# Where the folded sums of a feed-forward layer's last down run are added: behind the last split pair of the loop, with mixed and plain pairs alternating to the end

## The chip, the cores and the metric

The kernel runs on one core of a Trainium2 chip. Five engines take part, each with its own list of instructions that it works through in order: TensorE (PE; its weight loads are shown apart as PEld), VectorE (DVE), ScalarE (ACT), GpSimd (POOL, which here mainly issues accumulating loads) and SyncE (SP, which issues most loads). Data lies in SBUF; matmuls accumulate in eight PSUM banks of 128 x 512 float32 each. The metric is the device time of one execution in microseconds, lower is better. The kernel before took 1833.16 us, the median of three runs (1832.65 to 1834.87).

## The reference

One layer of an encoder on 256 tokens of width 2048, all in float32: a feed-forward layer, a mixer (a gated recurrence and windowed attention side by side), and a second feed-forward layer. The change lies in the feed-forward layers, which the reference computes twice with different weights:

```python
def rms_norm(x, gain):
    xf = x.astype(jnp.float32)
    y = xf * lax.rsqrt(jnp.mean(xf * xf, axis=-1, keepdims=True) + EPS)
    return (y * gain.astype(jnp.float32)).astype(x.dtype)

def swiglu(x, w_gate_up, w_down):
    gate, up = jnp.split(x @ w_gate_up, 2, axis=-1)
    return (jax.nn.silu(gate) * up) @ w_down
...
    ff = swiglu(rms_norm(x, pre_norm_ffn1[layer]), w_ffn1_gate_up[layer], w_ffn1_down[layer])
    x = x + 0.5 * rms_norm(ff, post_norm_ffn1[layer])
    ...
    ff = swiglu(rms_norm(x, pre_norm_ffn2[layer]), w_ffn2_gate_up[layer], w_ffn2_down[layer])
    x = x + 0.5 * rms_norm(ff, post_norm_ffn2[layer])
```

The inner width is 5632, so the down projection multiplies 256 x 5632 with 5632 x 2048.

## The kernel before

Each float32 operand is held as two parts, h (a rounded copy, made by a cast on ScalarE, line 176) and l (what is left, a subtraction on VectorE, line 177). A product is three matmuls: h with h, h with l, l with h. Making h and l of half a weight tile is called a split here; the split of one half is one cast of 128 x 1024 and one subtraction of 128 x 1024.

The down projection is done in two runs, one for each half of the 2048 output columns. In a run the four blocks of the result (two halves of the tokens times two halves of 1024 columns) stay in four PSUM banks, c (two named pa, two named pb). The 5632 rows of the weight matrix are taken as 22 pairs of 128 rows, numbered 0 to 21. A plain pair takes 8 products (24 matmuls) and two splits. A mixed pair (the even ones from 0 to 18) is multiplied by a scheme of seven products in place of eight: 21 matmuls, but three splits of 1024, one of 512, sums of weight blocks on VectorE (lines 1262 and 1263) and sums of the left operand (tile sp). Four of its seven products go to four further banks, p, for all mixed pairs of a run together. Behind the last mixed pair of a run the sums of p have to be added to the banks c. This is the fold: one copy on ScalarE (line 528) and eight additions on VectorE (lines 529, 522, 523 and 526 make the sums; 535, 539, 543 and 545 add them to the four banks). A later matmul into a bank has to wait for that bank's addition.

Most of the feed-forward layer stands inside a manual schedule: the instructions of each engine keep the order of the source. A table of pair numbers for each run (line 1199) gives the order of the pairs. In a step of the loop (lines 1321 to 1340) the next pair's splits stand ahead of this pair's products on ScalarE and VectorE (`splits`, line 1240); accumulating loads for a mixed pair are issued by POOL four steps ahead (`prepare`, line 1230); a raw weight tile is loaded again by SP as soon as its last split is done (`load_down`, line 1213). Splits write into a ring of five buffers for h and five for l, which come free when TensorE has used them.

The last two pairs of the second run, 20 and 21, are held: `finish` (line 707) loads and splits them into buffers of their own (the pool `post`), and then takes their products bank by bank, so that the norm of the first bank's results can start while the others are computed. This part up to the products is outside the manual schedule; there a scheduler places the instructions. In the first feed-forward layer `finish` also loads and splits the first two weight tiles of the next stage (`lead`, w_mix_in).

In the kernel before, the second run ends with the pairs 16, 1, 18, 17, 19 and then 20, 21. The last mixed pair is 18. The pair behind it, 17, is taken bank by bank, and the fold stands behind 17 and ahead of 19 (`play`, below). `Pairs` also serves the mixer's output projection, with other tables; there nothing changes.

Of the kernel before, what the change touches and what calls it, by code (L numbers as in the profile page):

```python
# [37 lines left out]
def hymba_layer_kernel(  # L38
# [37 lines left out]
    def nm(s):  # L76
        uid[0] += 1
        return f"{s}_{uid[0]}"
# [62 lines left out]
    def load(src, between=None, pool=rawp, **kw):  # L141
        raw = pool.tile([P, 2048], F32, tag="raw", name=nm("raw"), **kw)
        if len(src.shape) == 4:

            dst = raw.rearrange("p (a n b) -> p a n b", a=src.shape[1], n=src.shape[2])
            parts = [(dst[:, a], src[:, a]) for a in range(src.shape[1])]
        else:
            parts = [(raw.rearrange("p (a b) -> p a b", a=src.shape[1]), src)]
        for i, (to, of) in enumerate(parts):
            if i and between:  # L150
                between()
            nc.sync.dma_start(to, of)
        return raw

    def split_load(src, hp=hip, lp=lop, between=None, middle=None):
        return split(load(src, between), hp, lp, middle)

    def split(raw, hp=hip, lp=lop, middle=None):
        hs, ls = [], []
        for i in range(2):  # L160
            if i and middle:
                middle()
            h, l = split_half(raw, i, hp, lp)
            hs.append(h)
            ls.append(l)
        return hs, ls
# [31 lines left out]
    def close_far():  # L198
        far["cm"].__exit__(None, None, None)
# [132 lines left out]
    class LeadN:  # L332


        def __init__(self, w, c0, slot):
            self.w, self.c0, self.slot = w, c0, slot
# [259 lines left out]
    class Pairs(Blocks):  # L596
# [3 lines left out]

        HELD = 2
        firsts = 2

        def __init__(self, w, orders, tiles, sums, room, gain_src, keep=(), near=()):

# [94 lines left out]
        def second_run(self):  # L700
# [3 lines left out]
                    self.gains(m, n)  # L704
            self.run(1)

        def finish(self, mul, post, new_x=None, gain=None, lead=None):


            order = self.orders[1]  # L710
            n_order = len(order)
            self.post = post
            self.work(n_order - self.HELD)
            held = []
            for u in order[n_order - self.HELD :]:
                held.append((u, *split_load(self.source(u), hp=post, lp=post)))
            close_far()
            self.half_gain(post)
            if new_x:
# [4 lines left out]
            r = [None, None]  # L724
# [142 lines left out]
    NU = DFF // 256  # L867
# [139 lines left out]
    def ffn(gated, w_dn, post_gain, again, gain=None, lead=None, aside=None):  # L1007

        with ExitStack() as st:
# [108 lines left out]
            def some(steps, n):  # L1118
                for _ in range(n):
                    next(steps)  # L1120
# [61 lines left out]
            def pair_ahead(g, u):  # L1182
# [16 lines left out]
            orders = [  # L1199
                [9, 11, 8, 13, 10, 15, 12, 1, 0, 3, 14, 5, 16, 17, 2, 7, 4, 19, 6, 18, 20, 21],  # L1200

                [2, 7, 4, 9, 6, 11, 8, 13, 10, 12, 15, 0, 5, 14, 3, 16, 1, 18, 17, 19, 20, 21],
            ]
            added = {0: (12, 0, 14, 16, 2, 4, 6, 18), 1: (2, 4, 6, 10, 12, 0, 14, 16, 18)}
            steps = [(r, u) for r in range(2) for u in orders[r]][: 2 * NU - Pairs.HELD]
            in_order = sorted(
                (i - 3.5 if u in added[r] else i, i) for i, (r, u) in enumerate(steps)
            )
# [1 line left out]
            raws, firsts, got = {}, {}, {}  # L1210
            rows = None
# [26 lines left out]
                    )  # L1238

            def splits(i):  # L1240
                if i >= len(steps):
                    return
                r, u = steps[i]
                raw = raws[i]
                parts = got[i] = []
                b11, b12, b21, b22 = blocks(raw)
                if u not in MIXED:
                    parts.append(split_half(raw, 0))
                    yield
                    parts.append(split_half(raw, 1))  # L1250
                    load_down(raw)
                    yield
                    return
                four = raw.rearrange("p (i c) -> p i c", i=4)
                if i not in firsts:
                    first_block(i)
                    nc.vector.tensor_tensor(
                        four[:, 0:2], four[:, 0::3], four[:, 1:2].to_broadcast([P, 2, 512]), ALU.add
                    )
                parts.append(split_half(raw, 1))  # L1260
                rows.left_sums_ahead(u)
                nc.vector.tensor_tensor(b22, b11, b22, ALU.add)
                nc.vector.tensor_tensor(b21, b22, b21, ALU.add)
                yield
                parts.append(split_half(raw, 0))
                yield
                parts.append(split_half(raw, 1))
                load_down(raw)
                yield

            def products(i, among=None):
                r, u = steps[i]
                rows.pos = i - r * NU
                del raws[i]
                if u in MIXED:
                    rows.products(u, firsts.pop(i), *got.pop(i))
                else:
                    rows.play(u, *zip(*got.pop(i)), among)
                rows.pos += 1
# [3 lines left out]
            with tc.manual_schedule():  # L1283
                gated.prepare(1, MIXED_IN[0])
                some(gated.splits(1, 0), 2)
                for g in range(1, NG):
                    first_pairs(g, waiting)
                    for u in range(2, last - 1):
                        pair_ahead(g, u)
                    some(gated.splits(g, last), 2)  # L1290
                    if g < NG - 1:
                        gated.prepare(g + 1, MIXED_IN[0])
                    for one in gated.take(g, last - 1):
                        one()
                    boundary(g, gated.splits(g + 1, 0) if g < NG - 1 else splits(0))
                    waiting = units(gated.c, rest)
                    some(waiting, 2)
                room_cm.__exit__(None, None, None)
                close_far()
                back_cm = tc.tile_pool(name=nm("hb"), bufs=AWAY // 2, reuse_waits="tile")  # L1300
                back = back_cm.__enter__()
                fetch_at = {2: (1,), 3: (0,), 5: (3,), 6: (5,), 9: (2,), 10: (7,), 11: (4,), 13: (6,)}
                fetch_at.update({25: (0,), 26: (5,), 28: (3,), 29: (1,)})
                again_at = {8: 16, 14: 18}
                for u in MIXED[8:]:
                    sums[u] = None
                rows = Pairs(w_dn, orders, hts, sums, work, post_gain, near=MIXED[:2])
                rows.firsts = 3
                some(waiting, 2)
                ahead = splits(1)  # L1310
                some(ahead, 2)
                products(0)
                for _ in range(2):
                    load_down(back.tile([P, 2048], F32, tag="raw", name=nm("raw"), bufs=2))
                some(waiting, 1)
                ahead = splits(2)
                some(ahead, 2)
                some(waiting, 1)
                some(ahead, 1)
                products(1)  # L1320
                for i in range(2, len(steps)):
                    if i == NU + 18:
                        back_cm.__exit__(None, None, None)
                        early_cm.__exit__(None, None, None)
                        post = rows.post = st.enter_context(post_pool())
                    ahead = splits(i + 1)
                    next(ahead, None)
                    prepare(i + 4)
                    for u in fetch_at.get(i, ()):
                        fetch(u)  # L1330
                    next(ahead, None)
                    products(i)
                    for _ in ahead:
                        pass
                    if i in again_at:
                        sums[again_at[i]] = sums_again(again_at[i])
                    if i == 8:
                        rows.half_gain(far["pool"])
                    if i == NU - 1:
                        rows.second_run()  # L1340
            return rows.finish(
                mul=0.5, post=post, new_x=again, gain=gain and gain(), lead=lead
            )
# [8 lines left out]
    with tc.manual_schedule():  # L1352
# [9 lines left out]
        raw = rawp.tile([P, 2048], F32, tag="raw", name=nm("raw"))  # L1362
# [23 lines left out]
        raws = [load(gated.source(1))]  # L1386
# [97 lines left out]
    with ExitStack() as s2:  # L1484
# [398 lines left out]
        orders = [[0, 1, 4, 6, 5, 7, 2, 3], [0, 4, 1, 5, 6, 7, 2, 3]]  # L1883
        rows = Pairs(w_mix_out[0], orders, yt, ysums, yroom, post_norm_mix)
        rows.half_gain(far["pool"])
        rows.first_run()
        post = s2.enter_context(post_pool())
# [81 lines left out]
```

## Time and profile before

| | |
|---|---|
| median of three runs | 1833.16 us |
| profiled execution | 1832.72 us |
| its span, first to last instruction | 1830.9 us |
| PE busy | 1812.4 us, 99% of the span |
| PEld busy | 1503.5 us, 82% |
| DVE busy | 1599.2 us, 87% |
| ACT busy | 1130.9 us, 62% |
| POOL busy | 155.5 us, 8% |
| granted TensorE clock, mean | 0.998 |
| DMA | 444.45 MB, mean 243 GB/s |

The profile is that of one execution, whose time is 0.44 us under the median; the 1.8 us between its time and its span lie ahead of the first and behind the last instruction. Busy time of PE is time with a matmul in flight, so 99% tells only that it seldom stood empty. In a row of a timeline the first number is the start in microseconds from the span's start, the second the length; a number in brackets is how long the engine had been idle before, with what ended the wait. Lines are those of the kernel before; behind the change the same statements stand on lines up to 24 higher.

### The profile page before, as it was taken

Reading aid. Unit: us, or ns where it says so; the run is one execution under the profiler, and the core shown is the slowest. Engines: PE = TensorE matmul, PEld = TensorE weight load, DVE = VectorE, ACT = ScalarE, POOL = GpSimd, SP = SyncE. Lnnn points to the kernel's source line nnn. Section 1 sums busy time; section 2 is a strip of 40 time slices with the busy share of each in tenths; the row PEclk is TensorE's granted clock in tenths of the full one; section 3 lists DMA queues with packets and bytes.
Section 4 is the critical chain, followed back from the end, with each engine's and each line's share of the span. In section 5 each row is a group of like instructions: output and inputs, shape, how many; then the busy total and the mean of one; then the engine's idle time right before and its main releaser. Section 6 shows DMA issues by size and latency. Waiting matters only on the chain.

```text
span 1830.9 us, 23436 instructions
## 1 busy us (share of the span) xinstructions
PE 1812.4 (99%) x8438; PEld 1503.5 (82%) x8438; DVE 1599.2 (87%) x2041; ACT 1130.9 (62%) x1496; POOL 155.5 (8%) x149
## 2 busy tenths in 40 slices
PE   9999999999999999999999999999999999999997
PEld 6888888888888887888888888788888888888886
DVE  7999999999989988477687798899999999998986
ACT  6565666665656666476587556556666666566663
POOL 1011111111011100000000000001111111011110
PEclk9999999999999999999999999999999999999999
DMA  8789999998698985555554456789999888699892
GB/s 301 230 231 289 275 280 255 252 262 242 231 341 267 301 263 192 187 191 165 169 166 150 170 210 245 218 244 266 282 273 270 255 245 253 199 345 290 272 328 106
DMA packets 210420, 444.45 MB, mean 243 GB/s; under 512 B 11656, under 2 KB 46560, under 8 KB 209536
## 3 DMA queue, kind: packets, MB, share of 16 engines
q1 hardware_dynamic: 180032, 385.14, 60.2%
q0 software_dynamic: 30272, 57.82, 18.2%
q8 instruction: 66, 1.08, 0.2%
q14 instruction: 50, 0.41, 0.1%
HBM read 430.31 MB, written 12.60 MB: 242 GB/s over the span
## 4 chain that ended last, share of the span: by engine, by line
PE 89%; DVE 4%; ACT 3%; DMA 2%; issue 2%; POOL 0%; SPq 0%; DVEq 0%; ACTq 0%; POOLq 0%
PE pa L441 39%; PE pb L441 33%; PE pa L309 5%; PE pa L314 3%; PE pa L364 2%; PE pa L363 2%; PE pa L362 2%; DVE l L177 2%; DMA raw<-in_w_ffn_gate_up_dram 2%; ACT h L176 1%; PE pa L1100 1%; PE pb L1100 1%; PE pb L1690 0%; PE pb L1664 0%; PE pb L1768 0%
## 5 line engine op out<-in xcount | busy, mean ns | idle before, releaser
L176 ACT CAST h<-raw 128x1024 fp32r<-128x1024 f32 (+1 forms) x861 | 851.0, 1013 | 467.6 <-PE pb L441 154.5
L177 DVE TENSOR_TENSOR l<-raw,h 128x1024 fp32r<-128x1024 f32 (+1 forms) x861 | 983.8, 1173 | 140.2 <-ACT h L176 106.0
L441 PE MATMUL pa<-h,xt 128*128 128x512 f32 x1104 | 387.9, 392 | 0.1
L441 PE MATMUL pb<-h,xt 128*128 128x512 f32 x952 | 340.7, 392 | 0.5 <-DVE pb L1152 0.4
L441 PEld LDWEIGHTS pa<-h,xt 128*128 128x128 f32 x1104 | 207.2, 188 | 44.2 <-DVE xt L232 0.6
L441 PE MATMUL pa<-l,xt 128*128 128x512 f32 x552 | 216.0, 391 | 0.1
L441 PEld LDWEIGHTS pb<-h,xt 128*128 128x128 f32 x952 | 178.7, 188 | 43.6 <-DVE pb L1159 3.9
L441 PE MATMUL pb<-l,xt 128*128 128x512 f32 x476 | 185.6, 390 | 0.0
L441 PE MATMUL pa<-h,ht 128*128 128x512 f32 x464 | 163.1, 390 | 3.8 <-DVE pa L535 3.8
L441 PE MATMUL pb<-h,ht 128*128 128x512 f32 x464 | 163.0, 390 | 0.0
L936 POOL DMA_DIRECT2D raw<-in_w_ffn_gate_up_dram x76 | 92.0, 1211 | 738.5 <-DVE l L177 647.0
L309 PE MATMUL pa<-xt,h 128*128 128x512 f32 x512 | 124.5, 393 | 0.2 <-ACT h L176 0.2
L441 PEld LDWEIGHTS pa<-l,xt 128*128 128x128 f32 x552 | 103.8, 188 | 21.5 <-DVE l L177 1.7
L309 PEld LDWEIGHTS pa<-xt,h 128*128 128x128 f32 x512 | 93.8, 188 | 18.6 <-ACT h L176 0.6
L441 PE MATMUL pa<-h,xs 128*128 128x512 f32 x304 | 108.9, 389 | 0.0
L441 PE MATMUL pb<-h,xs 128*128 128x512 f32 x304 | 106.0, 389 | 0.0
L441 PEld LDWEIGHTS pa<-h,ht 128*128 128x128 f32 x464 | 87.1, 188 | 22.6 <-issue 4.6
L441 PEld LDWEIGHTS pb<-l,xt 128*128 128x128 f32 x476 | 89.5, 188 | 17.0
L441 PEld LDWEIGHTS pb<-h,ht 128*128 128x128 f32 x464 | 87.1, 188 | 18.0
L441 PE MATMUL pa<-l,ht 128*128 128x512 f32 x232 | 90.4, 390 | 0.0
L441 PE MATMUL pb<-l,ht 128*128 128x512 f32 x232 | 90.3, 389 | 0.0
L1234 POOL DMA_DIRECT2D raw<-in_w_ffn_down_dram x34 | 41.2, 1211 | 366.2 <-DVE la L177 345.9
(287 smaller groups left out, 2550.8 us busy)
## 6 DMA issues: line engine op xcount, KB each, us to landing
raw<-in_w_ffn_gate_up_dram SPq DMA_DIRECT2D x350, 512.0 KB, 5.8
raw<-in_w_ffn_down_dram SPq DMA_DIRECT2D x88, 1024.0 KB, 7.9
raw<-in_w_mix_in_dram SPq DMA_DIRECT2D x52, 1024.0 KB, 4.9
raw<-in_w_ffn_gate_up_dram POOLq DMA_DIRECT2D x76, 512.0 KB, 8.4
raw<-in_w_ffn_down_dram POOLq DMA_DIRECT2D x34, 512.0 KB, 10.1
raw<-in_w_mix_out_dram SPq DMA_DIRECT2D x16, 1024.0 KB, 5.0
ht<-away SPq DMA_DIRECT2D x24, 512.0 KB, 10.5
away<-ht SPq DMA_DIRECT2D x16, 512.0 KB, 6.8
```

The lines of the kernel that those rows point to most:

```text
L176: nc.scalar.copy(hi, src)
L177: nc.vector.tensor_tensor(lo, src, hi.bitcast(F32), ALU.subtract)
L309: nc.tensor.matmul(slot[f], weights(hs, kk, f), xcol(xt, k), start=(k == 0), stop=(k == KT - 1))
L314: nc.tensor.matmul(slot[f][:, 0:T], weights(ls, kk, f), xcol(xt, kh * 8 + kk, 0), start=False, stop=False,)
L362: nc.tensor.matmul(dst, xh, h[:, o : o + n], start=(k == 0), stop=False)
L363: nc.tensor.matmul(dst, xh, l[:, o : o + n], start=False, stop=False)
L364: nc.tensor.matmul(dst, xl, h[:, o : o + n], start=False, stop=(k == KT - 1))
L441: nc.tensor.matmul(self.bank(at), lhs, rhs, start=(n == 1), stop=n in (ends, self.of[at]), skip_group_check=n > ends,)
L936: nc.gpsimd.dma_start(raw[:, 0:1024].rearrange("p (k c) -> p k c", k=2), self.source(u, g)[:, :, 1], accum_op=ALU.add,)
L1100: nc.tensor.transpose(bank[:, o : o + P], zs[m][:, k * P : (k + 1) * P], ident)
L1234: nc.gpsimd.dma_start(raws[i][:, 0:1024].rearrange("p (k c) -> p k c", k=2), Pairs.part(w_dn, u, r)[:, :, 512:1024], accum_op=ALU.add,)
```

## The change

Three things are changed, all in the second down run of the feed-forward layers. The table of the second run is rewritten so that mixed and plain pairs alternate to the end (10, 15, 12, 5, 0, 3, 14, 1, 16, 17, 18, 19). With 18 in the place before last of the loop, pair 19 is the one taken bank by bank, and the fold stands behind pair 19, ahead of the held pairs. And the held pairs join the loop's list of loads, and their splits get fixed places inside the manual schedule (`hold`): those of pair 20 ahead of pair 18's products, those of pair 21 inside the fold, behind the addition to the first bank.

```diff
+        def hold(self, n, raw=None):
+
+            self.held = self.held or []
+            order = self.orders[1]
+            for _ in range(n):
+                u = order[len(order) - self.HELD + len(self.held)]
+                raw = raw or load(self.source(u))
+                self.held.append((u, *split(raw, hp=self.post, lp=self.post)))
+                raw = None
+
+        def fold_after(self, pos):
+
+            self.after = pos
+            self.rest = 6 * (len(self.order) - pos - 1)
...
             self.work(n_order - self.HELD)
-            held = []
-            for u in order[n_order - self.HELD :]:
-                held.append((u, *split_load(self.source(u), hp=post, lp=post)))
+            if self.held is None:
+                self.hold(self.HELD)
+            held = self.held
...
-                [2, 7, 4, 9, 6, 11, 8, 13, 10, 12, 15, 0, 5, 14, 3, 16, 1, 18, 17, 19, 20, 21],
+                [2, 7, 4, 9, 6, 11, 8, 13, 10, 15, 12, 5, 0, 3, 14, 1, 16, 17, 18, 19, 20, 21],
...
-            steps = [(r, u) for r in range(2) for u in orders[r]][: 2 * NU - Pairs.HELD]
+            steps = [(r, u) for r in range(2) for u in orders[r]]
...
             def splits(i):
-                if i >= len(steps):
+                if i >= 2 * NU - Pairs.HELD:
                     return
...
-                for i in range(2, len(steps)):
+                for i in range(2, 2 * NU - Pairs.HELD):
...
                     next(ahead, None)
+                    if i == NU + 18:
+                        rows.hold(1, raws[2 * NU - 2])
                     products(i)
...
                     if i == NU - 1:
                         rows.second_run()
+                        rows.fold_after(NU - Pairs.HELD - 1)
+                fold = rows.fold()
+                some(fold, 2)
+                rows.hold(1, raws[2 * NU - 1])
+                for _ in fold:
+                    pass
```

The three places at which this is seen in the built program are given for the first layer; in the second the same rows stand in the same order, without the next stage's loads.

VectorE around the fold, before. The tile raw_4212 holds pair 17, raw_635 pair 19, raw_5873 pair 20 and raw_5883 pair 21; y is the buffer of the sums, pa_5107 and pa_5108 are the first two banks c.

```order
L177 TENSOR_TENSOR l_5777<-raw_4212,h_5776 128x1024
L177 TENSOR_TENSOR l_5807<-raw_635,h_5806 128x1024
L177 TENSOR_TENSOR l_5876<-raw_5873,h_5875 128x1024
L177 TENSOR_TENSOR l_5811<-raw_635,h_5810 128x1024
L529 TENSOR_TENSOR y_5838<-pb_5127,y_5838 128x512
L177 TENSOR_TENSOR l_5880<-raw_5873,h_5879 128x1024
L522 TENSOR_TENSOR y_5838<-pb_5128,y_5838 128x512
L177 TENSOR_TENSOR l_5886<-raw_5883,h_5885 128x1024
L523 TENSOR_TENSOR y_5838<-pa_5126,y_5838 128x512
L526 TENSOR_TENSOR y_5838<-pa_5126,y_5838 128x512
L535 TENSOR_TENSOR pa_5107<-pa_5107,y_5838 128x512
L539 TENSOR_TENSOR pa_5108<-pa_5108,y_5838 128x512
```

VectorE there after the change, from pair 18's last split on; raw_629 holds pair 18 and then pair 21, raw_632 pair 19, raw_635 pair 20.

```order
L177 TENSOR_TENSOR l_5802<-raw_629,h_5801 128x1024
L177 TENSOR_TENSOR l_5812<-raw_632,h_5811 128x1024
L177 TENSOR_TENSOR l_5816<-raw_632,h_5815 128x1024
L177 TENSOR_TENSOR l_5820<-raw_635,h_5819 128x1024
L177 TENSOR_TENSOR l_5824<-raw_635,h_5823 128x1024
L529 TENSOR_TENSOR y_5872<-pb_5127,y_5872 128x512
L522 TENSOR_TENSOR y_5872<-pb_5128,y_5872 128x512
L523 TENSOR_TENSOR y_5872<-pa_5126,y_5872 128x512
L526 TENSOR_TENSOR y_5872<-pa_5126,y_5872 128x512
L535 TENSOR_TENSOR pa_5107<-pa_5107,y_5872 128x512
L177 TENSOR_TENSOR l_5880<-raw_629,h_5879 128x1024
L177 TENSOR_TENSOR l_5884<-raw_629,h_5883 128x1024
```

The five additions up to L535 now stand together, with the splits of 19 and 20 ahead of them and those of 21 behind; L539, L543 and L545 follow these.

TensorE at the bank whose addition is L535, before: the last products of pair 17 (ht_3557), then the first of pair 19 (ht_3902), which wait for L535.

```order
L441 MATMUL pb_5110<-h_5776,ht_3557 128x512
L441 MATMUL pb_5110<-l_5777,ht_3557 128x512
L441 MATMUL pb_5110<-h_5776,ht_3557 128x512
L441 MATMUL pa_5107<-h_5806,ht_3902 128x512
L441 MATMUL pa_5107<-l_5807,ht_3902 128x512
L441 MATMUL pa_5107<-h_5806,ht_3902 128x512
```

And after: the last products of pair 19, then the first of pair 20 (ht_4242), which now wait for L535.

```order
L441 MATMUL pb_5110<-h_5815,ht_3902 128x512
L441 MATMUL pb_5110<-l_5816,ht_3902 128x512
L441 MATMUL pb_5110<-h_5815,ht_3902 128x512
L441 MATMUL pa_5107<-h_5819,ht_4242 128x512
L441 MATMUL pa_5107<-l_5820,ht_4242 128x512
L441 MATMUL pa_5107<-h_5819,ht_4242 128x512
```

The wait moved behind pair 19, that is behind 24 more matmuls than have to come after pair 18.

SP's loads at the end of the run, before (pairs 19, 20, 21, the norm's gain row, then the next stage):

```order
L1218 DMA raw_635<-in_w_ffn_down_dram 128x2x1024
L152 DMA raw_5873<-in_w_ffn_down_dram 128x2x1024
L152 DMA raw_5883<-in_w_ffn_down_dram 128x2x1024
L661 DMA pg_5894<-in_post_norm_ffn_dram 128x1024
L152 DMA raw_5899<-in_w_mix_in_dram 128x4x512
```

And after:

```order
L1234 DMA raw_632<-in_w_ffn_down_dram 128x2x1024
L1490 DMA X_5894<-in_x_dram 128x2048
L1234 DMA raw_635<-in_w_ffn_down_dram 128x2x1024
L662 DMA pg_5892<-in_post_norm_ffn_dram 128x1024
L1234 DMA raw_629<-in_w_ffn_down_dram 128x2x1024
L152 DMA raw_5897<-in_w_mix_in_dram 128x4x512
```

The gain row moved ahead of pair 21's load, and half of the reload of X stands between the loads of 19 and 20. Pair 21 is loaded into the tile of pair 18 in both programs, so its load waits for pair 18's last split; behind pair 18 came two more pairs of the loop before, and comes one now. The next stage's first two loads wait for the last splits of 19 and 20, before for those of 19 and of 20 as well; its third waits for pair 21's.

More of the change, by code (lines that the diff above doesn't have):

```diff
@@ L602, in hymba_layer_kernel @@
         firsts = 2
+        held = None
         def __init__(self, w, orders, tiles, sums, room, gain_src, keep=(), near=()):
```

## The prediction

> **What bounds the kernel now.** I read the page's busy times first, then TensorE's waits, then TensorE's own timeline at the longest of them. Page and waits:
>
> ```profile
> span 1830.9 us, 23436 instructions
> ```
>
> ```profile
> PE pa L441 <- DVE pa L535: 3.8, 2, 1.9
> ```
>
> ```profile
> 594.00:687.00 93.00, 93.00 (x412) 77.06 (x411) 81.84 (x87) 59.91 (x68) 8.48 (x7) 1.00 0.89 284
> ```
>
> The second fence is a stretch of the first feed-forward layer's second down run: length, then busy time (instructions) of PE, PEld, DVE, ACT, POOL, then TensorE's clock, the DMA engines' share and GB/s. TensorE is busy for all 93 us. So the middle of the run offers nothing; only the wait on L535 does, once per feed-forward layer, 1.9 us each. L535 adds the first folded sum to bank (0,0); ahead of it stands pair 17, behind it pair 19. TensorE's rows around it, in both layers:
>
> ```profile
> 687.12 0.39 PE L441 MATMUL pb<-l,ht 128*128 128x512 f32 x1
> 687.35 0.39 PE L441 MATMUL pb<-h,ht 128*128 128x512 f32 x1
> 689.66 0.47 PE L441 MATMUL pa<-h,ht 128*128 128x512 f32 x1 [1.92 <-DVE pa L535]
> ...
> 692.50 0.39 PE L441 MATMUL pb<-h,ht 128*128 128x512 f32 x1
> ...
> 1803.42 0.39 PE L441 MATMUL pb<-h,ht 128*128 128x512 f32 x1
> 1805.73 0.47 PE L441 MATMUL pa<-h,ht 128*128 128x512 f32 x1 [1.92 <-DVE pa L535]
> ...
> 1808.55 0.39 PE L441 MATMUL pb<-h,ht 128*128 128x512 f32 x1
> ```
>
> ```profile
> 667.34 2.72 PE pa L441 x12
> ...
> 672.10 1.36 PE pa L441 x6
> ...
> 677.54 2.05 PE pa L441 x9
> ```
>
> Matmuls start 0.23 us apart (687.12 to 687.35), twelve take 2.72 (chain of waits). From the chain's starts a mixed pair takes 672.10 - 667.34 = 4.76 us and a plain pair 677.54 - 672.10 = 5.44.
>
> Why L535 is late, from VectorE's timeline (pair 18's third split to L535), and the same sums in the first run, where no split stands between them:
>
> ```profile
> 673.63 3.65 DVE L177 TENSOR_TENSOR l<-raw,h 128x1024 fp32r<-128x1024 f32 x3
> 678.72 1.23 DVE L177 TENSOR_TENSOR l<-raw,h 128x1024 fp32r<-128x1024 f32 x1 [1.44 <-ACT h L176]
> 680.75 3.50 DVE L177 TENSOR_TENSOR l<-raw,h 128x1024 fp32r<-128x1024 f32 x3 [0.80 <-ACT h L176]
> 684.16 0.69 DVE L529 TENSOR_TENSOR y<-pb,y 128x512 f32<-128x512 f32 x1
> 684.76 1.22 DVE L177 TENSOR_TENSOR l<-raw,h 128x1024 fp32r<-128x1024 f32 x1
> 685.89 0.69 DVE L522 TENSOR_TENSOR y<-pb,y 128x512 f32<-128x512 f32 x1
> ...
> 687.62 0.69 DVE L523 TENSOR_TENSOR y<-pa,y 128x512 f32<-128x512 f32 x1
> ...
> 688.82 0.69 DVE L535 TENSOR_TENSOR pa<-pa,y 128x512 f32<-128x512 f32 x1
> ```
>
> ```profile
> 581.47 0.68 DVE L529 TENSOR_TENSOR y<-pb,y 128x512 f32<-128x512 f32 x1
> ...
> 584.11 0.69 DVE L535 TENSOR_TENSOR pa<-pa,y 128x512 f32<-128x512 f32 x1
> ```
>
> The end of pair 18 to the end of pair 17 is one plain pair, 5.44 us. In it VectorE ran three splits ahead of the sums and two more between them; L529 to the end of L535 took 5.35 us instead of the first run's 3.33.
>
> **The change, part by part.** It removes and adds no instruction; each engine has as many as before.
>
> *The gap.* Ahead of pair 19 both programs have ten mixed and nine plain pairs, so TensorE reaches it at the same time, 687.35 + 0.23 = 687.58, but now waits there for no sum. Gap removed: 689.66 - 687.58 = 2.08. The twelve matmuls after it took 692.50 - 689.66 = 2.84, 0.12 above 2.72. Together 2.20. Second layer: 1805.73 - (1803.42 + 0.23) = 2.08, and 1808.55 - 1805.73 = 2.82, 0.10 too long: 2.18. Sum 4.38 us, if the sums are now on time.
>
> The clock through the gap, then ScalarE's casts, SP's last loads, and (last line) how long SP's six loads of 675 to 712 took to land:
>
> ```profile
> 684.00:690.00 6.00, 4.08 (x19) 3.10 (x18) 6.00 (x9) 2.65 (x4) 0.00 (x0) 1.00 0.79 275
> ```
>
> ```profile
> 677.63 1.05 ACT L176 CAST h<-raw 128x1024 fp32r<-128x1024 f32 x1 [1.67 <-PE pb L441]
> 679.66 2.95 ACT L176 CAST h<-raw 128x1024 fp32r<-128x1024 f32 x3 [0.98 <-PE pa L441]
> 682.52 0.57 ACT L528 COPY y<-pa 128x512 f32<-128x512 f32 x1
> ...
> 689.29 2.00 ACT L176 CAST h<-raw 128x1024 fp32r<-128x1024 f32 x2 [3.35 <-DMA raw<-in_w_mix_in_dram]
> 698.14 0.60 ACT L685 ACTIVATE jk<-pa 128x512 bf16<-128x512 f32 x1 [6.86 <-PE pa L441]
> ```
>
> ```profile
> 676.17 0.37 SPq L152 DMA_DIRECT2D raw<-in_w_ffn_down_dram  x1
> 684.27 2.10 SPq L152 DMA_DIRECT2D raw<-in_w_mix_in_dram  x2
> ```
>
> ```profile
> DMA to landing us min/median/max: 4.8/5.1/6.6
> ```
>
> The granted clock is 1.00 across the gap, so I put the 0.12 and 0.10 down to the stop itself, not to a slower clock, and let them go with it. The Trainium skill (TensorE: Matmul & The Clock Gate, "What's actually happening") has the clock halved only after an idle window of about 3.4 us; by it a gap of 2.08 costs no clock, which the 1.00 confirms, and a sum of gaps alone would be 4.16 us, 1829.0.
>
> *Are the sums on time?* Pair 18 now stands one plain pair later, so I shift its rows by 5.44. Its third split ended when pair 21's load was issued (676.17): 681.61. Pair 19's second split: 678.72 + 5.44 = 684.16, done 685.39. Pair 20's casts follow 19's on ScalarE (677.63 + 5.44 + 1.05 = 684.1; two at about 0.95 each, from 2.95 for three): 686.0, and the copy L528 ends at 686.6. Pair 20's two splits at 1.14 each (3.50 for three) end at 687.6, then the five sums, 3.33: L535 ends at 690.9. From L535's end (688.82 + 0.69) to TensorE's start (689.66) passed 0.15: 691.1. TensorE wants the bank after pair 19's 24 matmuls, 687.58 + 5.44 = 693.02. Cover 1.9 us; if it goes, every microsecond comes back as the old gap.
>
> *Pair 21's splits between L535 and L539.* They hold up three sums. L539 ends at 690.9 + 2 x 1.14 + 0.7 = 693.9; its bank is wanted twelve matmuls after 693.02, at 695.74: cover 1.8. The splits themselves are wanted six matmuls in, at 694.38 and 695.06, and end at 692.0 and 693.2. This holds if pair 21 has landed. Its load is issued at 681.61 and its first cast is free to run from 686.6: a landing of 5.1 hides. On SP's queue the gain row now stands ahead of this load, but waits only for the last read of pair 0, long past. Pair 20's load goes out behind pair 1's second split: such a split ends 2.4 us after the next pair starts (678.72 + 1.23 against 677.54), and pair 16 starts at 687.58 - 4.76 - 5.44 - 4.76 = 672.62, so 675.0, 9.1 us ahead of its cast. Cost 0.
>
> *The first layer's end.* The next stage's first two loads now wait for pair 19's and 20's second splits, 685.4 and 687.6 (before: 684.27 and about 686.0), and their casts stand ahead of the first square, which comes at 698.14 - 2.20 = 695.9; with the longest landing, 6.6, the first is cast at 694.0. VectorE reaches the first lead split after L545, at 695.1, and ends the second at 697.4, 0.7 past the place the gain product wants; the second square is 2.72 after the first, so this hides. The third load is the nearest thing:
>
> ```profile
> 692.46 0.37 SPq L152 DMA_DIRECT2D raw<-in_w_mix_in_dram  x1
> ...
> 702.45 1.05 ACT L176 CAST h<-raw 128x1024 fp32r<-128x1024 f32 x1
> ```
>
> It waits for pair 21's splits, 693.2, and its cast moves to 702.45 - 2.20 = 700.25: 7.05 us, against a longest landing of 6.6. Cost 0. The second layer has no such stage behind it.
>
> *The middle: 15 and 12, 0 and 5, 14 and 3, 16 and 1, 18 and 17 swap.* The bound for a gain is 0 (TensorE has no wait there). For a loss: POOL's accumulating loads keep their order and their three pairs' distance, and VectorE meets one mixed pair at a time where 10 and 12 were neighbours. I take 0; what hides it is that distance, and its price is in the last rival.
>
> Sum: 4.38 us. Against the profiled execution, 1832.72 (span 1830.9): 1828.34. The runs' median is 0.44 above it: 1833.16 - 4.38 = 1828.8. With a measurement telling about 0.2% (3.7 us) from no change, the ceiling lies only 0.7 beyond it.
>
> **The rivals.** *Late last pair.* ScalarE and VectorE stand still at pair 21 until its load lands, and L539, L543, L545 stand behind. Casts 2.0, second split 1.2, L539 and its signal 0.85: landing plus 4.0 must be under 695.74, that is 10.1 us after 681.61. For it: row 689.29, where ScalarE stood 3.35 us on a load; and the second layer's other down loads, the slowest of which took 11.6 (min, median, max):
>
> ```profile
> DMA to landing us min/median/max: 4.9/8.0/11.6
> ```
>
> Against it: this load's own place showed 6.6 or less. At 11.6 each layer loses 1.5: 1833.16 - 4.38 + 3.0 = 1831.8. The Trainium skill (PSUM — Partial Sum Buffer, "Engine vs sequencer instructions") calls the queues of ScalarE and VectorE strict FIFO; by that rule no later sum could pass the waiting split, which is this rival, and row 689.29 agrees.
>
> *First layer's gain lost at the lead.* If the third load takes over 7.05, its split stands ahead of the next stage's first operands on VectorE, and the lateness goes to TensorE: from 9.25 on the first layer gains nothing, 1833.16 - 2.18 = 1831.0. Against it: 6.6; for it: only 0.45 us of room.
>
> *Slower: the middle becomes bound by DMA.* Pair 18's accumulating load on POOL, the first sum on VectorE that needs it, the DMA share between (the 1.06), and how long all accumulating down loads took to land:
>
> ```profile
> 657.88 1.21 POOL L1234 DMA_DIRECT2D raw<-in_w_ffn_down_dram  x1 [9.03 <-DVE la L177]
> ```
>
> ```profile
> 672.31 0.68 DVE L1262 TENSOR_TENSOR raw<-raw 128x512 f32<-128x512 f32 x1
> ```
>
> ```profile
> 665.00:670.00 5.00, 5.00 (x24) 4.14 (x23) 3.31 (x3) 2.33 (x3) 0.00 (x0) 1.00 1.06 331
> ```
>
> ```profile
> DMA to landing us min/median/max: 6.1/10.1/12.3
> ```
>
> Pair 18's accumulating load has 672.31 - 657.88 = 14.4 us; such loads land in 12.3 at most, so 2.1 are left, in a stretch where the DMA engines are full. The reload of X moves with pair 14's splits, up to 5.44 later, into the next loads. Lateness x costs TensorE x - 2.1 per layer; from x = 4.3 the kernel is slower than before, from 6.1 by over 0.2%, 1836.9 and more. Against it: pair 18's load moves by the same 5.44, so the distance stays.
>
> **How the numbers follow.** Forecast (both gaps go): 0.68, of which 0.08 measure within 0.2%, the ceiling being so near. Late last pair 0.10, first layer's gain lost 0.10, both within 0.2%. Slower 0.12. So faster 0.60, same 0.28, slower 0.12. Predicted 1828.8. The range begins at 1827.6 (1.2 below, about the spread of the runs before) and goes to 1832.4, to take in 1831.0 and 1831.8.
>
> **What would show it.** Right: TensorE's waits name no L535; L529 to L535 stand in one piece of 3.3 us on VectorE, ending about 2 us ahead of pair 20's first matmul; pair 19 follows pair 18 without a gap. Wrong: TensorE waiting on L539 or on a split of pair 21 (late load); a wait on L364 or L210 grown after the first layer (lead); or waits on L177 or sp inside the run (DMA). A residue of 0.3 us of the old wait would say that pair 20's splits were later than shifted.

## The result, and the profile after

The changed kernel takes 1827.05 us, the median of seven runs (1826.91 to 1827.87), where the kernel before took 1833.55 in seven runs beside it (1831.67 to 1835.30). The ratio is 0.9965, 95% interval 0.9953 to 0.9976: a gain of 6.5 us, by the interval 4.4 to 8.6. The forecast was faster by 4.4 us, 1828.8, in a range from 1827.6. The direction was right, and the time lies 0.55 us below the range. Two things in these numbers are to be explained: the surplus of about 2 us, and that the changed kernel's runs lie within 1.0 us of each other and those of before 3.6 apart.

The profiled execution of the changed kernel took 1826.96 us. Its span, and its longest waits of TensorE:

```profile
span 1825.2 us, 23437 instructions
```

```profile
PE pb L130 <- DVE idle L124: 1.4, 1, 1.4
PE pa L1116 <- DVE s L1096: 0.9, 1, 0.9
PE pb L1857 <- ACT pt L1849: 0.8, 1, 0.8
```

The wait on L535 (3.8 us in two pieces before) is gone, and none of the three longest that are left belongs to a down run. VectorE's timeline at the first layer's fold:

```profile
683.88 3.50 DVE L177 TENSOR_TENSOR l<-raw,h 128x1024 fp32r<-128x1024 f32 x3 [1.44 <-ACT h L176]
687.29 0.68 DVE L529 TENSOR_TENSOR y<-pb,y 128x512 f32<-128x512 f32 x1
688.01 0.69 DVE L522 TENSOR_TENSOR y<-pb,y 128x512 f32<-128x512 f32 x1
688.73 0.69 DVE L523 TENSOR_TENSOR y<-pa,y 128x512 f32<-128x512 f32 x1
689.34 0.68 DVE L526 TENSOR_TENSOR y<-pa,y 128x512 f32<-128x512 f32 x1
689.94 0.69 DVE L535 TENSOR_TENSOR pa<-pa,y 128x512 f32<-128x512 f32 x1
690.54 2.35 DVE L177 TENSOR_TENSOR l<-raw,h 128x1024 fp32r<-128x1024 f32 x2
692.80 0.69 DVE L539 TENSOR_TENSOR pa<-pa,y 128x512 f32<-128x512 f32 x1
```

The five sums stand in one piece of 3.34 us and end at 690.63. TensorE's rows where pair 19 ends and pair 20 begins, in the first layer and in the second:

```profile
692.51 0.39 PE L441 MATMUL pb<-h,ht 128*128 128x512 f32 x1
692.74 0.39 PE L441 MATMUL pa<-h,ht 128*128 128x512 f32 x1
...
1805.35 0.39 PE L441 MATMUL pb<-h,ht 128*128 128x512 f32 x1
1805.57 0.39 PE L441 MATMUL pa<-h,ht 128*128 128x512 f32 x1
```

The steps are 0.23 and 0.22 us: no gap in either layer, with 2.11 us between L535's end and the matmul that needs it in the first.

Where the 5.70 us between the two profiled spans come from is read by laying the same matmul of both traces side by side. The lead of the changed kernel, worked out from the starts, changes at these places and stays flat between them:

| place | lead behind it, us | step |
|---|---|---|
| first loads, up to 98 us | 0.33 | +0.33 |
| first layer's fold | 2.48 | +2.15 |
| L278, start of the second layer (1156 us) | 3.85 | +1.37 |
| transposes at 1177 us | 3.48 | -0.37 |
| second layer's fold | 5.70 | +2.22 |

Two steps are the gaps of the prediction. The third is a wait that was there in the profile of before alone (TensorE's wait, then the rows of ScalarE and of VectorE that lead to it):

```profile
PE pb L278 <- DVE dg L277: 1.1, 1, 1.1
```

```profile
1154.39 1.57 ACT L176 CAST h<-raw 128x512 fp32r<-128x512 f32 x2 [2.27 <-DMA raw<-in_w_ffn_gate_up_dram]
```

```profile
1155.65 0.28 DVE L277 TENSOR_SCALAR dg<-ident,scales 128x128 f32<-128x128 f32 x1
```

A gate-up load landed late, the cast waited 2.27 us for it, and L277 stands behind that cast's subtraction. Whether this belongs to the old kernel or to one execution was the first question.

### The profile page after: what moved, and what is told of

The parts are those of the page before. It is cut to its first block, busy times and chain, and to the rows that moved or that the text cites. A ratio compares the mean times of both kernels' runs of the same rounds, so it can differ in the third digit from the quotient of the medians.

```text
span 1825.2 us, 23437 instructions
## 1 busy us (share of the span) xinstructions
PE 1811.7 (99%) x8438; PEld 1503.5 (82%) x8438; DVE 1600.3 (88%) x2041; ACT 1131.9 (62%) x1496; POOL 155.5 (9%) x149
## 4 chain that ended last, share of the span: by engine, by line
PE 95%; ACT 2%; DVE 2%; DMA 1%; issue 0%; POOL 0%; DVEq 0%; SPq 0%; ACTq 0%; POOLq 0%
PE pa L441 41%; PE pb L441 36%; PE pa L309 5%; PE pa L314 3%; PE pa L364 2%; PE pa L363 2%; PE pa L362 2%; DVE l L177 1%; PE pa L1116 1%; PE pb L1116 1%; DMA raw<-in_w_ffn_gate_up_dram 0%; ACT h L176 0%; PE pb L1714 0%; PE pb L1688 0%; PE pb L1792 0%
```

## The experiments

Theory A: the gaps are all, and the rest is what single executions differ in. Theory B: the old order causes the rest, by the wait on L277. Both kernels were profiled and timed again, and the change was made in one layer at a time. The one-layer kernels are the changed kernel with the table, the list of loads and the fold chosen by layer (the diff is that of the first layer alone; for the second the condition is `lead is None`):

```diff
+            moved = lead is not None
...
-                [2, 7, 4, 9, 6, 11, 8, 13, 10, 15, 12, 5, 0, 3, 14, 1, 16, 17, 18, 19, 20, 21],
+                [2, 7, 4, 9, 6, 11, 8, 13, 10, 15, 12, 5, 0, 3, 14, 1, 16, 17, 18, 19, 20, 21]
+                if moved
+                else [2, 7, 4, 9, 6, 11, 8, 13, 10, 12, 15, 0, 5, 14, 3, 16, 1, 18, 17, 19, 20, 21],
...
```

**The kernel before again.** 

> The kernel before, profiled and timed a second time. Theory A: the two gaps at L535 (2.2 us each) are all that the change takes away, and the rest of the difference between the medians (6.5 against 4.4 us) is what single executions of the kernel before differ in. Then the new profile shows both gaps again, 1.9 us each, but the 1.1 us for which TensorE waited on L277 at 1155 us need not stand there. Theory B: that wait belongs to the order of the kernel before. Then it stands in the new profile too, at 1.0 to 1.2 us. The time is 1831.5 to 1835 us by either.

**The changed kernel again.** 

> The changed kernel, profiled and timed a second time. Theory A: no wait on L535; a wait on L277 of about 1 us may stand in it or not, as in the kernel before. Theory B: no wait on L277 over 0.5 us. Time 1827 to 1828 us by either; runs that lie further apart than 1.5 us would speak for A.

**First layer alone.** 

> The change in the first feed-forward layer alone. Theory A: one gap of 2.2 us goes, so about 1831.2 us against 1833.4 (ratio 0.9988), and the second layer's L535 keeps its 1.9 us. Theory B, with the surplus tied to the earlier start of what follows the first layer: 2.2 + 2.1 = 4.3 us, about 1829.1 us (ratio 0.9977).

**Second layer alone.** 

> The change in the second feed-forward layer alone. Theory A: one gap of 2.2 us goes, about 1831.2 us (ratio 0.9988), the first layer's L535 keeps its 1.9 us. Theory B with the surplus tied to the first layer: the same 1831.2; with the surplus made in the second layer itself: 4.3 us, 1829.1 us. If each layer is worth 3.2 us by itself, the gaps are mis-sized in both.

| kernel | median us | runs | ratio to before, 95% |
|---|---|---|---|
| before (beside these) | 1833.91 | 28, 1832.23 to 1836.17 | |
| before again | 1834.05 | 11, 1832.17 to 1837.67 | 1.0002 (0.9993 to 1.0011) |
| changed again | 1828.23 | 6, 1827.59 to 1828.76 | 0.9969 (0.9957 to 0.9980) |
| first layer alone | 1830.57 | 11, 1829.89 to 1833.67 | 0.9984 (0.9975 to 0.9993) |
| second layer alone | 1831.63 | 11, 1830.05 to 1832.54 | 0.9988 (0.9979 to 0.9997) |

The wait on L277 of 1.1 us is not in the second profile of before, nor at that size in any other here: it was that execution's, and B falls. The layers add up (3.3 + 2.3 = 5.6 against 5.7 for both), with intervals too wide to say that they differ. But with 28 and 6 runs 5.7 us remain, 1.3 more than the gaps. The interval, 3.7 to 7.9 us, does not exclude 4.4 by itself, so the times alone do not refute A; the profile of the kernel with the second layer alone shows a cost that A leaves out. TensorE's timeline at its untouched first-layer gap:

```profile
687.61 0.39 PE L441 MATMUL pb<-h,ht 128*128 128x512 f32 x1
689.91 0.47 PE L441 MATMUL pa<-h,ht 128*128 128x512 f32 x1 [1.92 <-DVE pa L535]
690.22 0.40 PE L441 MATMUL pa<-l,ht 128*128 128x512 f32 x1
690.45 0.83 PE L441 MATMUL pa<-h,ht 128*128 128x512 f32 x2
...
691.51 1.05 PE L441 MATMUL pa<-h,ht 128*128 128x512 f32 x2
692.36 0.63 PE L441 MATMUL pa<-l,ht 128*128 128x512 f32 x1
...
694.34 0.40 PE L441 MATMUL pb<-h,ht 128*128 128x512 f32 x1
```

The same 1.92 us of wait, but then matmuls 0.43 us apart instead of 0.23: the twelve behind the gap take 694.34 - 689.91 = 4.43 us, where the profile of before had 2.84 and an undisturbed stretch 2.72. The stretches of the same place (after the busy times of the five engines comes the granted clock):

```profile
689.00:690.00 1.00, 0.09 (x1) 0.12 (x2) 1.00 (x3) 0.38 (x1) 0.00 (x0) 1.00 0.98 322
690.00:691.00 1.00, 1.00 (x4) 0.85 (x5) 1.00 (x3) 1.00 (x2) 0.00 (x0) 0.86 1.02 385
691.00:692.00 1.00, 1.00 (x4) 0.72 (x3) 1.00 (x2) 0.61 (x1) 0.00 (x0) 0.50 0.65 250
...
693.00:694.00 1.00, 1.00 (x3) 0.78 (x3) 1.00 (x2) 0.00 (x0) 0.00 (x0) 0.50 0.27 31
694.00:695.00 1.00, 1.00 (x5) 0.79 (x4) 0.95 (x1) 0.00 (x0) 0.00 (x0) 0.94 0.73 184
```

The clock is at half speed for 3.41 us and then full again, which costs 4.43 - 2.84 = 1.6 us more than the gap in the first profile of before. The second profile of before has the same at its second-layer gap and not at its first, the kernel with the first layer alone at its second-layer gap; the first profile of before had it at neither. In the clock records of each trace the half-speed stretches begin a whole number of 3.413 us windows after the clock's first full moment (in the kernel with the first layer alone, full from 10.36: at 1177.72, 342 windows, and at 1805.77, 526 windows). So a third theory: **C**, a gap has a second price, a half-speed window behind it, in those executions where enough of it falls inside one window of this grid. Where the grid lies differs from execution to execution, which would also make the spread of before. The mean granted clock that each run lists bears this out. One such window lowers it by 0.5 x 3.41/1831 = 0.0009; over the 83 timed runs of the kernel before for which it is listed (it is rounded to 0.001, and counts every half-speed window, wherever it stands):

| mean clock | runs | mean time us |
|---|---|---|
| 0.999 | 24 | 1832.64 |
| 0.998 | 34 | 1833.77 |
| 0.997 | 19 | 1835.15 |
| 0.996 | 6 | 1836.20 |

**The gap kept, but filled.** If C is right, work of no use in the gap must make the kernel faster, though pair 19 starts no earlier.

```diff
             if self.pos == self.after + 1 and not self.within:
                 for _ in self.fold():
                     pass
+                for _ in range(self.fill[self.now]):
+                    nc.tensor.matmul(
+                        self.p[0], self.tiles[u][:, 0, 0, 0:P], hs[0][:, 0:512], start=True, stop=True
+                    )
...
+                rows.fill = (0, 8)
```

> The kernel before with eight matmuls of no use (into a bank p whose sum has been copied) between pair 17 and pair 19 of the second run, in both layers: 8 x 0.227 = 1.8 us of work in a gap of 2.08, so that pair 19 still waits for L535 and the gap itself costs what it did. Theory C: the gap has a second price, a clock window of 3.41 us at half speed behind it in those executions in which the idle time falls into one window (1.7 us each). Filled, the idle time is 0.3 us and no window is halved: about 1832.4 us, near the lowest runs of before, and runs within about 1.5 us of each other. Rival: the surplus has nothing to do with the clock; then it takes what before takes, 1833.9 us with runs 4 us apart.

Measured: 1832.79 us (11 runs, 1832.51 to 1834.27) beside 1833.98 for before (23 runs, 1831.90 to 1836.06); ratio 0.9994 (0.9985 to 1.0003). TensorE's rows at the first layer's gap, and the clock of four microseconds from there in each layer:

```profile
688.74 1.97 PE L582 MATMUL pa<-h,ht 128*128 128x512 f32 x8
690.73 0.50 PE L441 MATMUL pa<-h,ht 128*128 128x512 f32 x1
```

```profile
690.00:694.00 4.00, 3.98 (x18) 2.94 (x17) 4.00 (x7) 2.00 (x2) 0.00 (x0) 1.00 0.64 242
...
1807.00:1811.00 4.00, 4.00 (x19) 3.30 (x18) 1.99 (x3) 0.00 (x0) 0.00 (x0) 1.00 0.00 0
```

The eight matmuls at L582 fill the gap, the first matmul of pair 19 still comes 690.73 - 688.74 = 2.0 us late, and the clock stays at 1.00. The median is 1.2 us lower and the spread 1.8 instead of 4.2, as C has it; the interval of the ratio by itself still takes in 1.

**Half filled.** The same with `rows.fill = (0, 4)`. 

> As the filled gap, with four matmuls of no use in place of eight: about 1.0 us of idle time is left ahead of pair 19 in each layer. Theory C, in which it takes about 1.5 to 1.9 us of idle time in one window to halve the next: no half window, so as with eight, 1832.8 us and runs within 2 us. If 1 us of idle time is enough, or if any gap can cost a half window: 1833.5 to 1834 us, with half windows in the profile.

Measured: 1832.55 us (11 runs, 1832.20 to 1833.90), before 1834.24 beside it (21 runs); ratio 0.9993 (0.9984 to 1.0002). TensorE's rows:

```profile
688.18 1.07 PE L582 MATMUL pa<-h,ht 128*128 128x512 f32 x4
690.17 0.50 PE L441 MATMUL pa<-h,ht 128*128 128x512 f32 x1 [0.92 <-DVE pa L535]
```

0.92 us of idle time fell inside one window in both layers, and neither was followed by half speed. The second price is not one of every gap.

**A longer gap.**

```diff
             add(y12, p6, y11, ALU.add)
+            for _ in range(self.more[self.now]):
+                add(y22, p7, y12, ALU.add)
...
+                rows.more = (0, 2)
```

> The kernel before with the addition of L522 kept waiting by two more additions of the same shape on VectorE in each second run's fold (their result is overwritten). With them one more split moves ahead of L535, so it comes about 2 x 0.65 + 1.14 = 2.4 us later: gaps of about 4.5 us. Theory C: idle time of 4.3 us always fills enough of one window, so the clock is halved behind both gaps in every execution: 1832.7 + 2 x 2.4 + 2 x 1.7 = 1840.9 us, less where part of the half window falls into the gap itself. Without a second price: 1834 + 4.8 = 1838.8 us.

Measured: 1841.72 us (5 runs, 1840.01 to 1842.13), ratio 1.0039 (1.0027 to 1.0052). TensorE's row at the first layer's gap (L538 is L535 in this kernel), and the clock behind each gap:

```profile
693.10 0.77 PE L442 MATMUL pa<-h,ht 128*128 128x512 f32 x1 [4.25 <-DVE pa L538]
```

```profile
691.00:692.00 1.00, 0.00 (x0) 0.00 (x0) 1.00 (x3) 1.00 (x2) 0.00 (x0) 0.63 1.00 377
...
694.00:695.00 1.00, 1.00 (x4) 0.71 (x4) 1.00 (x3) 0.00 (x0) 0.00 (x0) 0.50 0.99 379
695.00:696.00 1.00, 1.00 (x4) 0.81 (x3) 1.00 (x2) 0.00 (x0) 0.00 (x0) 0.50 0.69 240
...
1814.00:1815.00 1.00, 1.00 (x5) 0.76 (x4) 1.00 (x2) 0.00 (x0) 0.00 (x0) 0.62 0.00 0
1815.00:1816.00 1.00, 1.00 (x4) 0.81 (x3) 0.02 (x1) 0.00 (x0) 0.00 (x0) 0.50 0.07 16
...
1817.00:1818.00 1.00, 1.00 (x4) 0.80 (x3) 0.00 (x0) 0.00 (x0) 0.00 (x0) 0.67 0.00 0
```

Both gaps are followed by half speed, and the time is 0.8 us above what C said, 2.9 above the sum without a second price. In the first layer half speed lasts two windows, from 691.26 to 698.08, the first of which lies partly in the gap itself; in the second layer it lasts one. The twelve matmuls behind the gaps take 5.14 and 4.41 us, 2.3 and 1.6 more than the 2.84 and 2.82 of before: 3.9 in all in this execution, where C had counted 3.4. The rest of the 0.8 is within the spread of the five runs.

The mean clocks of the timed runs say the same over many executions. Of the 83 of the kernel before, 25 lie at 0.997 or lower. Of the 47 runs of the kernels without a long gap there (the changed kernel, the two filled ones, and the next two below) none does; with one gap left it is 4 of 11 in each layer, with the two longer gaps all 5.

Left is which part of the change brings the gain. **The old order with the fold in one piece:** old table, fold behind 17, both held pairs' splits behind all its sums.

```diff
...
-                    if i == NU + 18:
-                        rows.hold(1, raws[2 * NU - 2])
...
-                        rows.fold_after(NU - Pairs.HELD - 1)
-                fold = rows.fold()
-                some(fold, 2)
+                rows.hold(1, raws[2 * NU - 2])
                 rows.hold(1, raws[2 * NU - 1])
-                for _ in fold:
-                    pass
```

> The old order of the pairs, with the fold where it stood (behind 17, ahead of 19), but the splits of 20 and 21 placed by the source behind all its sums, so that L529 to L535 stand in one piece. Theory: three splits (1.14 us each) less lie ahead of L535, so it ends at about 689.5 - 3 x 1.14 = 686.1, ahead of the 687.6 at which TensorE wants the bank. No gap, no half window: the whole gain without a new table, 1828.2 us (ratio 0.9969). Rival, that the alternation of the pairs is what helps: the gap shrinks by part of it only, 1830 us or more.

Measured: 1828.48 us (6 runs, 1828.36 to 1829.14), ratio 0.9970 (0.9958 to 0.9981): all of the gain. VectorE's rows, then TensorE's first matmul of pair 19:

```profile
683.63 0.68 DVE L529 TENSOR_TENSOR y<-pb,y 128x512 f32<-128x512 f32 x1
...
686.28 0.69 DVE L535 TENSOR_TENSOR pa<-pa,y 128x512 f32<-128x512 f32 x1
```

```profile
688.00 0.39 PE L441 MATMUL pa<-h,ht 128*128 128x512 f32 x1
```

L535 ends at 686.97, 0.9 us later than expected but 1.0 us ahead of its use. The new table is not needed for the gain.

**The new order with the splits left free:** new table and fold behind 19, the held pairs loaded and split by `finish` as before.

```diff
-            steps = [(r, u) for r in range(2) for u in orders[r]]
+            steps = [(r, u) for r in range(2) for u in orders[r]][: 2 * NU - Pairs.HELD]
...
-                    if i == NU + 18:
-                        rows.hold(1, raws[2 * NU - 2])
...
-                fold = rows.fold()
-                some(fold, 2)
-                rows.hold(1, raws[2 * NU - 1])
-                for _ in fold:
+                for _ in rows.fold():
                     pass
```

> The new order with the fold behind 19, but the held pairs' loads and splits left to the scheduler: one split of 21 stands between L522 and L523, those of 20 stand among the splits of 18. Theory: L535 ends at about 690.6, TensorE wants it at 692.9; no gap, 1828.2 us (ratio 0.9969), as with all of the change. Rival, that the places of the splits matter: a wait on L535 or on a split of 18 of 0.5 us or more in each layer, 1829.5 us or more.

Measured: 1828.27 us (6 runs, 1827.90 to 1828.89), ratio 0.9971 (0.9959 to 0.9982): again all of it. VectorE's rows and TensorE's first matmul of pair 20:

```profile
689.56 1.23 DVE L177 TENSOR_TENSOR l<-raw,h 128x1024 fp32r<-128x1024 f32 x1 [0.20 <-ACT h L176]
...
691.90 0.69 DVE L535 TENSOR_TENSOR pa<-pa,y 128x512 f32<-128x512 f32 x1
```

```profile
693.80 0.39 PE L441 MATMUL pa<-h,ht 128*128 128x512 f32 x1
```

A split does stand between the sums, but L535 ends at 692.59, 1.2 us early. Either way is enough by itself, the sums in one piece or the new table with the fold behind 19; the changed kernel, which has both, is no faster.

**The splits of 21 first.**

```diff
-                fold = rows.fold()
-                some(fold, 2)
                 rows.hold(1, raws[2 * NU - 1])
-                for _ in fold:
+                for _ in rows.fold():
                     pass
```

> The changed kernel with the splits of pair 21 ahead of the fold instead of inside it; in the first layer the scheduler also puts a split of the next stage between L522 and L523. This tests the cover of 1.9 us. First layer: L535 ends at 690.6 + 2.3 + 1.2 = 694.1 at the earliest, wanted at 692.9: a wait of about 1.4 us. Second layer: 1803.46 + 2.3 = 1805.8, wanted at about 1805.6: a wait of 0.2 to 0.5. Together 1.6 to 1.9 us over the changed kernel: about 1830.0 us on this chip. If the cover were larger than worked out: 1828.2.

Measured: 1830.80 us (11 runs, 1830.12 to 1832.52), ratio 0.9986 (0.9977 to 0.9995), 2.6 above the changed kernel where 1.6 to 1.9 were expected. VectorE's rows in the first layer, and TensorE's in both:

```profile
692.69 1.23 DVE L177 TENSOR_TENSOR l<-raw,h 128x1024 fp32r<-128x1024 f32 x1 [0.33 <-ACT h L176]
...
695.03 0.69 DVE L535 TENSOR_TENSOR pa<-pa,y 128x512 f32<-128x512 f32 x1
```

```profile
695.87 0.47 PE L441 MATMUL pa<-h,ht 128*128 128x512 f32 x1 [1.57 <-DVE pa L535]
...
1809.49 0.47 PE L441 MATMUL pa<-h,ht 128*128 128x512 f32 x1 [0.20 <-DVE pa L535]
```

The cover was sized rightly and goes where it was said. The first layer's wait came out longer than expected, because the next stage's split had to wait 0.33 us for its cast. Counted from the matmul step ahead, the two stops are 1.74 and 0.36 us, 2.1 in all; the other 0.5 between the medians is within the runs' spread and was not followed further.

**The middle alone.** Only the pairs 12 to 16 in the new order, everything from 18 on as before.

```diff
-                [2, 7, 4, 9, 6, 11, 8, 13, 10, 12, 15, 0, 5, 14, 3, 16, 1, 18, 17, 19, 20, 21],
+                [2, 7, 4, 9, 6, 11, 8, 13, 10, 15, 12, 5, 0, 3, 14, 1, 16, 18, 17, 19, 20, 21],
```

> The kernel before with the pairs 12, 15, 5, 0, 3, 14, 1, 16 in the new order, and the end of the run (18, 17, 19, 20, 21), the fold and the held pairs as they were. The prediction costed the middle at 0: 1834 us and the same waits on L535. If the middle were worth something, or cost something through the accumulating loads: away from 1834 by over 1 us, and a wait on L177, sp or L1262 inside the run.

Measured: 1834.31 us (11 runs, 1832.74 to 1836.52), ratio 1.0001 (0.9993 to 1.0010). Of TensorE's waits:

```profile
PE pa L441 <- DVE pa L535: 3.8, 2, 1.9
```

Both gaps are as they were, and the middle is worth nothing, as costed. This profile, too, has one gap with a half-speed window behind it and one without: of eight such gaps in five profiles, four had it.

## Why the prediction was right and where it was wrong

- *The gap, 2.20 and 2.18 us.* Right for the execution that was read: the traces show 2.15 and 2.22. Only the reason given for 0.12 and 0.10 of it, the stop, is not shown: with the gap filled and TensorE idle for almost none of it, the twelve matmuls behind it still take 693.62 - 690.73 = 2.89 us.
- *The sums are on time.* Right. L535 was put at 690.9 and ended at 690.63; pair 21's load was put at 681.61 and issued at 681.33; neither L539 nor pair 21's splits were waited for. The cover of 1.9 us, which allows 0.15 from L535's end to TensorE's start, measured 2.11 - 0.15 = 1.96, and the run with pair 21's splits first used it up.
- *The first layer's end and the middle, cost 0.* Right: no wait grew behind the first layer, and the middle alone gives 1.0001 (0.9993 to 1.0010).
- *The price of a gap: the step that failed.* "The granted clock is 1.00 across the gap, so I put the 0.12 and 0.10 down to the stop itself" is true of the one execution, and was then taken for every one, so the sum has no term for the clock. In others the clock is halved for 3.41 us behind the gap. The size: the filled gaps put the kernel with its gaps but without half windows at 1832.79 and 1832.55, and before beside them at 1833.98 and 1834.24, 1.2 and 1.7 us more. Each of the two intervals just takes in 1; the profiles and the mean clocks are what tie the difference to the half windows. So the gain is 4.4 + 1.2 to 1.7 = 5.6 to 6.1 us, and 5.7 was measured in the repeat. By the grid the share of executions can be estimated too, if it lies anywhere with equal chance: a gap of 1.92 us lies whole in a window of 3.41 in (3.41 - 1.92)/3.41 = 44% of them (four of eight had it), and 2 x 0.44 x 1.6 = 1.4 us.
- *What stays open.* Of the first comparison's 6.5 us, 0.4 to 0.9 stay over; with seven runs of before that lie 3.6 us apart, its interval does not tell this from nothing. The changed kernel's own median moved by 1.2 us, to 1828.23 in the repeat, which lies inside the range although the forecast's gain is 1.3 too small there as well; that is luck, for the median of three from which the forecast started, 1833.16, lies 0.4 to 1.1 us under the medians of before taken later. The two profiles of the changed kernel differ by 0.95 us at the first loads (up to 58 us) and by 0.47 at the transposes, both outside the change; why was not followed.
- *The range.* Its low end was set by the spread of the runs before, without asking what makes runs differ by 2 to 4 us in a kernel in which TensorE waits for 2 us twice. That spread was the sign of the missing term, and 1.5 us more below would have held the result.
- *The page that was weighed.* The Trainium skill (TensorE: Matmul & The Clock Gate, "What's actually happening") has the clock halved after at least one idle window of about 3.4 us, and calls the window free-running. The length of 3.41 us and the free-running grid agree with the traces; that a whole idle window is needed does not, since 1.92 us inside one were enough. The prediction took the rule as confirmed by a single 1.00, in an execution in which each gap lay across two windows of the grid (0.93 and 0.99 us of idle time in the first layer, 1.02 and 0.90 in the second).
- *The rivals.* None came about. Pair 21's load was not late in the changed kernel. In the run with its splits first ScalarE did wait for it, 0.44 us, and cast it 4.85 us after its issue (682.72 to 687.57), under the 5.1 that the prediction took. Row 689.29, named for this rival, shows ScalarE waiting for a load; whether something behind a waiting instruction could have passed it, that row does not show, since the next one there had to wait for TensorE.

## What to carry to other kernels

A wait of TensorE costs its length and, when most of a clock window falls into it, a stretch at half speed behind it; one profile shows only whether that happened once, so look at the spread of the times and at the mean granted clock of every run before pricing a gap at its length. Where a gap can't be closed, matmuls of no use in it can buy back the second part. And before an order is rewritten, look at what stands ahead of and inside the late chain of work: here to move three splits behind the sums, one from ahead of them and two from between them, was worth as much as the new table, and the two did not add.

## What the runs showed of the hardware

Behind such gaps TensorE's clock falls to half for whole windows of 3.413 us, on a grid whose place differs from execution to execution (its first full-speed moment lies 4.6 to 10.4 us after the span's start). At the gaps of L535, idle time within one window (worked out from the starts and ends of the matmuls, the ends as the profile models them, against the grid) of 1.92 us (four times) and more was followed by half speed, of 0.92, 1.27, 1.58 and 1.71 us not; in the kernel with the longer gaps a window with 1.84 us of idle time that was itself at half speed was followed by another. The sum of idle time is not the whole rule: at the transposes of 1177 us, 1.48 us were followed by half speed in one profile, and 1.63 not in another. What is counted there stays open.
